# Two attention layers with adaptive norms on one core: the gates spread by high and low parts, a room check by lifetimes, and another order table

## The chip, the cores and the metric

The kernel runs on one core of one Trainium2 chip. The metric is the device time of one execution in microseconds (us), read as the median of several runs; lower is better. The engines are TensorE (PE; PEld are its weight loads), VectorE (DVE), ScalarE (ACT), GpSimd (POOL) and SyncE (SP), which issues most of the transfers (DMA).

## The reference, cut to what matters

Two layers over x of 256 tokens by 1024 channels, all in F32. Each layer takes a shift, a scale and a gate from one conditioning vector c, applies a mixer (first a sparse attention with three branches, NSA, then a block attention, MoBA), and adds the gated result:

```python
cond = jax.nn.silu(c)
for i in range(DEPTH):                       # 2
    shift, scale, gate = jnp.split(cond @ ada_w[i] + ada_b[i], 3, axis=-1)
    h = rms_norm(x, norm_g[i]) * (1 + scale[:, None, :]) + shift[:, None, :]
    ...                                      # y = nsa_mixer(h, ...) or moba_mixer(h, ...)
    x = x + gate[:, None, :] * y

# both mixers, cut: projections of h, 16 heads of 64 in 4 groups, softmax attention, a gated output
q, k, v, z = split_cols(h @ w_in, ...)
q = partial_rope(rms_norm(q, q_g), cos, sin)
p = masked_softmax(q @ k * scale, mask)
o = p @ v
return (o * jax.nn.silu(z)) @ w_out
```

`gate` is one row of 1024 numbers for each layer. The first mixer has compressed keys and gates of its three branches besides.

## The kernel before

**Numbers as two parts.** The large products (h with `w_in`, the gated attention output with `w_out`) run in F32R, a type of TensorE that keeps fewer bits of an F32 number. For exactness each operand is cut into `hi` (the F32R cast, on ACT) and `lo` (the rest, a subtraction on DVE), and three products hi·hi, hi·lo and lo·hi are added up in PSUM. `parts_of` makes the two parts of a piece of weights; the tags `hi` and `lo` have four buffers each. Transposes, the softmax's products with values and the products for shift, scale and gate run on F32 operands.

**How the work is staged.** First comes the start: c, x and the first columns of `ada_w` and `w_in` are loaded in small pieces into tiles named `early`. c is transposed into `RT` and turned into `condz` (silu of c, one column for each block of 128 channels); shift and scale of layer 0 are products of `condz` with columns of `ada_w`; they make `HT`, the transposed h in two parts. Products with `w_in` give k, v and q; then the NSA attention by pairs of heads (`pair_a`: scores, masked maxima on DVE, exponentials on ACT, scaling on DVE, transposes on PE, products with values); the products with `w_out`; then the same for the second layer (`pair_b`). Beside the main line run `side` steps: shift and scale of layer 1, and the two gates.

**The gate.** `ada_gate(l)` sums the gate over the partitions' 128 channels at a time: a tile `gate` of 128x1024 is cleared, its first partition gets the bias, and eight `scalar_tensor_tensor` on DVE add a block of `ada_w`, scaled by a column of `condz`. What then is missing is the sum over the 128 partitions, and that on all of them: a product with `ones`, a 128x128 tile of 1.0, in two halves of 512 columns. Both operands are F32. ACT copies the result from PSUM back to `gate`, where `x_update` reads it at the layer's end.

**The order.** Nothing runs in the order of the code. Every call is recorded by `Plan` with its dependencies; `Plan.issue` then writes out each engine's queue by simulating clocks: of the operations that are ready on an engine it takes the one that can start first, by level and then by its number (its place in the code). `LATER_BY` shifts numbers (first, last, shift), so it says what goes ahead of what; `HOLD` keeps single operations back until a planned time. Both are tables of plain numbers that belong to this code's numbering: an operation that is added moves all later numbers.

**Tiles.** A tag is a set of buffers of one size. `Plan.tile` gives names; `issue` hands out buffers as operations come. A tile may be given ahead of its turn only if `_safe` says that all tiles in between still find a buffer.

Of the kernel before, what the change touches and what calls it, by code (L numbers as in the profile page):

```python
# [10 lines left out]
F32R = mybir.dt.float32r  # L11
# [6 lines left out]
P = 128  # L18
# [21 lines left out]
ISSUE, FIRST_BYTE, RATE, LANDED = 450.0, 1500.0, 315.0, 700.0  # L40

LATER_BY = [
# [11 lines left out]
]  # L54
SHIFT = {i: d for a, b, d in LATER_BY for i in range(a, b + 1)}
HOLD = {
# [3 lines left out]
}  # L60


# [10 lines left out]
class Plan:  # L73
# [158 lines left out]
    @staticmethod  # L232
    def _safe(tag, k):

        if k not in tag.known:
            held = tag.early | {k}
            end = max(tag.last[h] for h in held)
            tag.known[k] = all(
                sum(a not in held and a not in tag.done for a in tag.alive[b]) + len(held) <= tag.bufs
                for b in range(tag.next, len(tag.tiles)) if b not in held and b not in tag.given and tag.first[b] <= end)  # L240
        return tag.known[k]

# [191 lines left out]
def kernel(  # L434
# [25 lines left out]
    const = ctx.enter_context(tc.tile_pool(name="const", bufs=1))  # L460
    work = ctx.enter_context(tc.tile_pool(name="work", bufs=1))
    psum = ctx.enter_context(tc.tile_pool(name="psum", bufs=1, space=bass.MemoryType.PSUM))
    plan = Plan(nc)
    T, A, V, G, Q = plan.T, plan.A, plan.V, plan.G, plan.S
# [97 lines left out]
        keep(maskC[:, m, :], [[-16, 16]], m * P - 31)  # L562
    ones = const.tile([P, P], F32, name="ones")
    nc.gpsimd.memset(ones, 1.0)
    identR = const.tile([P, P], F32R, name="identR")
    V.tensor_copy(identR, identF)
    emask = const.tile([P, 2], F32, name="emask")
# [186 lines left out]
    def ada_gate(l):  # L754
# [5 lines left out]
        for kk in range(8):  # L760
            w = ada_piece(l, kk, 2 * D, D)[:, 0, :]
            with plan.at(FILL):
                V.scalar_tensor_tensor(gate, w, condz[:, kk, 0:1], gate, op0=OP.mult, op1=OP.add)
            yield
        for s in range(2):
            t = tile_of("ps", 512)
            with plan.at(FILL):
                T.matmul(t, ones, gate[:, s * 512:(s + 1) * 512], start=True, stop=True)
                A.copy(gate[:, s * 512:(s + 1) * 512], t)

    side = []
# [792 lines left out]
```

## Time and profile before

| what | value |
|---|---|
| median of 3 runs | 308.93 us (308.55 to 309.64) |
| the profiled execution | 308.65 us |
| its span, first to last instruction | 306.9 us |
| busy: PE, PEld | 297.4 us (97%), 242.4 us (79%) |
| busy: DVE, ACT, POOL | 248.6 us (81%), 203.0 us (66%), 29.3 us (10%) |
| granted clock of TensorE | 1.000 over the span |
| DMA | 65.80 MB, mean 214 GB/s |

All instructions that the plan writes out stand under one line (L406 in this kernel), since a helper issues them; so rows are told apart by their tiles, `out<-in`, in which buffer numbers are left out. `acc` and `ps` are PSUM tiles, `p` and `pT` the probabilities and their transposes, `qg` holds q and later the gated outputs, `tiny` the maxima and sums of rows. A matmul's modelled end can lie behind the start of the next one, so lengths of neighbours overlap and starts tell the pace.

### The profile page before, as it was taken

To read this page: it belongs to the slowest core of one execution; us is meant where nothing else is said; L and a number is where in the kernel's file an instruction comes from. 1 tells how busy PE (TensorE), PEld (TensorE's weight loads), DVE (VectorE), ACT (ScalarE), POOL (GpSimd) and SP (SyncE) were. 2 spreads that over 40 slices of the span, in tenths; PEclk is the share of its full clock that TensorE was granted. 3 is DMA by queue.
4 is the path that set the end of the run, shared out by engine and by line. 5 is a ranking of instruction groups with operands and counts; after the bars stand their busy time and mean duration, and the time that the engine had idled before them with its cause. 6 is when DMAs were issued, how large, how long until landed. Compare 5 with 4: busy or idle time off the path is not lost.

```text
span 306.9 us, 6115 instructions
## 1 busy us (share of the span) xinstructions
PE 297.4 (97%) x2097; PEld 242.4 (79%) x2097; DVE 248.6 (81%) x737; ACT 203.0 (66%) x484; POOL 29.3 (10%) x100
## 2 busy tenths in 40 slices
PE   3999999999999999999999999999999999999995
PEld 3866767878878696878897788787788999878784
DVE  2773473678699989799999898796599999999664
ACT  4644254674946786689877975866466589999510
POOL 8028980000000000000000000000000000000000
PEclk9999999999999999999999999999999999999999
DMA  7999999699974294958568259126487780531002
GB/s 249 323 357 368 367 355 336 220 260 328 351 273 143 64 379 149 346 193 347 147 199 266 76 185 326 41 75 209 142 259 228 242 275 15 142 138 66 2 34 103
DMA packets 41099, 65.80 MB, mean 214 GB/s; under 512 B 4220, under 2 KB 20970, under 8 KB 41068
## 3 DMA queue, kind: packets, MB, share of 16 engines
q1 hardware_dynamic: 40708, 65.36, 65.0%
q8 instruction: 16, 0.26, 0.3%
q14 instruction: 15, 0.12, 0.1%
q10 hardware_dynamic: 168, 0.06, 0.1%
q0 software_dynamic: 192, 0.00, 0.0%
HBM read 64.36 MB, written 1.05 MB: 213 GB/s over the span
## 4 chain that ended last, share of the span: by engine, by line
PE 83%; DVE 5%; ACT 5%; DMA 3%; issue 2%; ACTq 1%; DVEq 0%
PE ps L406 48%; PE acc L406 36%; DVE p L406 3%; ACT p L406 2%; DMA rot<-in_c_dram 1%; DMA raw<-in_nsa_w_out_dram 1%; DVE lo L406 1%; ACT pT L406 1%; ACT hi L406 1%; ACTq L406 1%; ACT n_out L406 1%; DVE tiny L406 0%; ACT qg L406 0%; DVE n_out L406 0%; ACT y L406 0%
## 5 line engine op out<-in xcount | busy, mean ns | idle before, releaser
L406 ACT CAST hi<-raw 128x1024 fp32r<-128x1024 f32 (+1 forms) x48 | 49.2, 1027 | 17.4 <-PE acc L406 15.0
L406 DVE TENSOR_TENSOR lo<-raw,hi 128x1024 fp32r<-128x1024 f32 (+1 forms) x48 | 56.5, 1183 | 3.3 <-ACT hi L406 3.0
L406 ACT ACTIVATE p<-p,tiny 128x128 f32<-128x128 f32 (+1 forms) x96 | 43.2, 460 | 10.8 <-DVE tiny L406 10.6
L406 PE MATMUL acc<-hi,HT 128*128 128x512 f32 (+1 forms) x160 | 49.6, 383 | 0.1
L406 PE MATMUL acc<-HT,hi 128*128 128x256 f32 x192 | 39.0, 288 | 0.0
L406 PEld LDWEIGHTS acc<-hi,HT 128*128 128x128 f32 x160 | 28.8, 188 | 7.0 <-issue 1.2
L406 DVE CUSTOM_DVE_ANT_0 p<-ps,causal 128x128 f32<-128x128 f32 (+1 forms) x96 | 30.8, 346 | 1.6 <-PE ps L406 1.5
L406 PEld LDWEIGHTS acc<-HT,hi 128*128 128x128 f32 x192 | 30.4, 188 | 0.9 <-issue 0.7
L406 PE MATMUL acc<-lo,HT 128*128 128x512 f32 (+1 forms) x80 | 30.3, 382 | 0.2 <-DVE lo L406 0.2
L406 PE MATMUL ps<-hi,HT 128*128 128x512 f32 (+1 forms) x96 | 28.9, 367 | 0.0
L406 PE MATMUL ps<-KTA,qg 128*128 128x256 f32 (+2 forms) x192 | 27.3, 282 | 0.0
L406 PE MATMUL acc<-HT,lo 128*128 128x256 f32 x96 | 27.3, 286 | 0.0
L406 PEld LDWEIGHTS ps<-KTA,qg 128*128 128x128 f32 x192 | 24.1, 189 | 3.4 <-issue 1.2
L406 PE MATMUL ps<-hi,qg 128*128 128x256 f32 (+1 forms) x96 | 24.4, 324 | 0.0
L406 PE MATMUL acc<-hi,qg 128*128 128x512 f32 x64 | 23.3, 415 | 0.0
L406 ACT COPY pT<-ps 128x384 f32<-128x384 f32 x48 | 21.1, 493 | 2.3 <-PE ps L406 2.1
L406 DVE TENSOR_TENSOR lo<-early,hi 128x1024 fp32r<-128x1024 f32 (+2 forms) x17 | 17.3, 1038 | 5.1 <-ACT hi L406 4.7
L406 PE MATMUL ps<-identF,p 128*128 128x128 f32 x144 | 21.1, 275 | 0.2
L406 PEld LDWEIGHTS ps<-hi,HT 128*128 128x128 f32 x96 | 17.2, 188 | 4.6 <-issue 1.9
L406 DVE SCALAR_TENSOR_TENSOR gate<-raw,condz,gate 128x1024 f32<-128x1024 f32 x16 | 20.4, 1276 | 0.4 <-DMA raw<-in_ada_w_dram 0.4
L406 ACT CAST hi<-early 128x1024 fp32r<-128x1024 f32 (+2 forms) x17 | 14.6, 895 | 8.5 <-DMA early<-in_nsa_w_in_dram 6.7
L406 PEld LDWEIGHTS ps<-identF,p 128*128 128x128 f32 x144 | 16.2, 140 | 3.9 <-DVE p L406 1.0
(218 smaller groups left out, 617.7 us busy)
## 6 DMA issues: line engine op xcount, KB each, us to landing
raw<-in_ada_w_dram SPq DMA_DIRECT2D x32, 512.0 KB, 4.6
raw<-in_moba_w_in_dram SPq DMA_DIRECT2D x20, 512.0 KB, 4.4
early<-in_ada_w_dram SPq DMA_DIRECT2D x12, 512.0 KB, 10.1
raw<-in_nsa_w_in_dram SPq DMA_DIRECT2D x12, 512.0 KB, 6.1
early<-in_nsa_w_in_dram SPq DMA_DIRECT2D x9, 512.0 KB, 9.2
raw<-in_nsa_w_out_dram SPq DMA_DIRECT2D x8, 512.0 KB, 4.5
raw<-in_moba_w_out_dram SPq DMA_DIRECT2D x8, 512.0 KB, 4.2
early<-in_nsa_w_in_dram SPq DMA_DIRECT2D x9, 256.0 KB, 4.8
```

Source lines behind the costliest of these rows:

```text
L406: r = getattr(self.engines[e], method)(*[self._real(a) for a in args], **{k: self._real(a) for k, a in kw.items()})
```

## The change

1. `ada_gate` spreads the gate by parts: `parts_of` cuts `gate` (as two halves of 512) into `hi` and `lo` in F32R, and for each half two F32R products, of `hi` and of `lo` with `onesR`, add up in one PSUM tile, in place of one F32 product. `onesR` is a new F32R copy of `ones`, made once on DVE. So eight products stand for four; one cast on ACT and one subtraction on DVE are added for each layer, and one cast on DVE at the start.
2. `_safe` counts room by lifetimes: a tile that is held ahead of its turn counts at a place only if it comes behind that place or is alive there.
3. `LATER_BY` and `HOLD` are other tables.

```diff
 LATER_BY = [
-    (110, 111, -64), (256, 256, 155), (308, 311, -51), (317, 318, -56), (331, 331, 298), (351, 351, 26),
...
+    (162, 163, -25), (347, 347, 181), (443, 472, -10), (604, 604, 15), (634, 641, 236), (643, 645, 124),
...
 HOLD = {
-    0: 3500, 121: 16500, 168: 22100, 306: 52600, 313: 37600, 384: 32300, 386: 34800, 391: 48600, 396: 51100,
...
+    91: 18000, 95: 15300, 308: 19200, 310: 22300, 314: 36200, 389: 47600, 391: 50700, 605: 50800, 1251: 146800,
...
@@ _safe
-                sum(a not in held and a not in tag.done for a in tag.alive[b]) + len(held) <= tag.bufs
+                sum(a not in tag.done for a in tag.alive[b]) + sum(h > b for h in held) <= tag.bufs
@@
     ones = const.tile([P, P], F32, name="ones")
     nc.gpsimd.memset(ones, 1.0)
+    onesR = const.tile([P, P], F32R, name="onesR")
+    V.tensor_copy(onesR, ones)
@@ ada_gate
+        hi, lo = parts_of(gate.rearrange("p (s n) -> p s n", s=2))
         for s in range(2):
             t = tile_of("ps", 512)
             with plan.at(FILL):
-                T.matmul(t, ones, gate[:, s * 512:(s + 1) * 512], start=True, stop=True)
+                with plan.group():
+                    T.matmul(t, onesR, hi[:, s], start=True, stop=False)
+                    T.matmul(t, onesR, lo[:, s], start=False, stop=True)
                 A.copy(gate[:, s * 512:(s + 1) * 512], t)
```

The tables move instructions nearly everywhere. Three places follow, with the queue before and the queue now. A number behind a tile's name is its buffer.

ACT's queue at the start: `rot` is the tile into which c is loaded, `y` takes the rows of norms and biases, `sg` is the sigmoid of c, `n_in` and `ss` the squares of x and their sums. Before:

```order
L406 DMA y_135<-in_norm_g_dram 16x128
L406 DMA y_135<-in_ada_b_dram 48x128
L406 DMA y_135<-in_nsa_cmp_b_dram 4x128
L406 DMA y_135<-in_nsa_cmp_pe_dram 32x128
L406 DMA rot_151<-in_c_dram 8x128
L406 ACT_TABLE_LOAD
L406 ACTIVATE n_in_155,ss_156<-X 128x1024
L406 ACTIVATE n_in_166,ss_167<-X 128x1024
L406 ACTIVATE sg<-RT 128x8
```

Now:

```order
L403 DMA rot_136<-in_c_dram 8x128
L403 DMA y_140<-in_norm_g_dram 16x128
L403 DMA y_140<-in_ada_b_dram 48x128
L403 DMA y_140<-in_nsa_cmp_b_dram 4x128
L403 DMA y_140<-in_nsa_cmp_pe_dram 32x128
L403 ACT_TABLE_LOAD
L403 ACTIVATE sg<-RT 128x8
L403 ACTIVATE n_in_162,ss_163<-X 128x1024
L403 ACTIVATE n_in_174,ss_175<-X 128x1024
```

The transfer of c has gone from the fifth place to the first, and `sg` from behind both squares of x to ahead of them; on DVE `condz` goes ahead of the row norms in the same way, behind the new cast of `onesR`.

PE's queue at the second layer's gate, amid the products of z (`acc<-HT,hi`), of the output (`acc<-hi,qg`) and the attention's scores (`ps<-KTA,qg`) and transposes (`ps<-identF,p`). Before:

```order
L406 MATMUL acc_272<-HT,hi_331 128x256
L406 MATMUL ps_153<-gate_357,ones 128x512
L406 MATMUL ps_232<-identF,p_722 128x128
L406 MATMUL ps_232<-identF,p_734 128x128 x2
L406 MATMUL ps_198<-gate_357,ones 128x512
L406 MATMUL acc_299<-hi_297,qg_1306 128x512
```

Now:

```order
L403 MATMUL acc_281<-HT,hi_345 128x256 x2
L403 MATMUL acc_275<-hi_328,qg_1406 128x512
L403 MATMUL ps_154<-hi_248,onesR 128x512
L403 MATMUL ps_154<-lo_342,onesR 128x512
L403 MATMUL acc_281<-HT,lo_271 128x256
L403 MATMUL acc_281<-HT,hi_345 128x256
L403 MATMUL acc_275<-lo_369,qg_1406 128x512
L403 MATMUL acc_275<-hi_328,qg_1406 128x512 x2
L403 MATMUL ps_154<-KTA,qg_1571 128x128 x4
L403 MATMUL ps_243<-hi_248,onesR 128x512
L403 MATMUL ps_243<-lo_342,onesR 128x512
```

The two products of the gate have become two pairs, they stand behind the first output products, and no transpose of `p` stands between them any more.

DVE's queue ahead of that gate: the last sums of `gate`, between the scaling of `p`, the sums' reciprocals (`tiny`), and the gated outputs (`g`, `qg`). Before:

```order
L406 SCALAR_TENSOR_TENSOR gate_357<-raw_637,condz,gate_357 128x1024
L406 SCALAR_TENSOR_TENSOR g_1000<-zT_736,ps_207 128x256
L406 SCALAR_TENSOR_TENSOR g_1022<-zT_736,ps_173 128x256
L406 RECIPROCAL tiny_1202<-tiny_1202 128x4
L406 TENSOR_SCALAR tiny_926<-tiny_926 128x4
L406 SCALAR_TENSOR_TENSOR gate_357<-raw_616,condz,gate_357 128x1024
L406 TENSOR_TENSOR qg_1306<-g_1000,qg_1306 128x256
L406 TENSOR_TENSOR qg_1306<-g_1022,qg_1306 128x256
L406 TENSOR_SCALAR p_722<-p_722,tiny_1202 128x128 x2
L406 TENSOR_SCALAR p_734<-p_734,tiny_1202 128x256
L406 SCALAR_TENSOR_TENSOR zT_727<-y_202,acc_299 128x512
L406 SCALAR_TENSOR_TENSOR zT_741<-y_135,acc_272 128x512
```

Now, where `lo<-gate` follows five rows further on:

```order
L403 SCALAR_TENSOR_TENSOR gate_350<-raw_605,condz,gate_350 128x1024
L403 TENSOR_TENSOR qg_1406<-g_1002,qg_1406 128x256
L403 TENSOR_TENSOR qg_1406<-g_1023,qg_1406 128x256
L403 RECIPROCAL tiny_1148<-tiny_1148 128x4
L403 RECIPROCAL tiny_1155<-tiny_1155 128x4
L403 SCALAR_TENSOR_TENSOR gate_350<-raw_622,condz,gate_350 128x1024
L403 TENSOR_SCALAR p_720<-p_720,tiny_1148 128x128 x2
L403 TENSOR_SCALAR p_734<-p_734,tiny_1148 128x256 x2
L403 TENSOR_SCALAR p_727<-p_727,tiny_1155 128x128 x2
L403 TENSOR_SCALAR p_722<-p_722,tiny_1155 128x256 x2
L403 SCALAR_TENSOR_TENSOR gate_350<-raw_656,condz,gate_350 128x1024
L403 TENSOR_TENSOR lo_369<-raw_650,hi_328 128x1024
```

Three sums of the gate stand here now, where two stood; the products with z (`zT`) have moved behind them.

More of the change, by code (lines that the diff above doesn't have):

```diff
@@ L56 @@
 HOLD = {
[3 rows of a table removed]
+    91: 18000, 95: 15300, 308: 19200, 310: 22300, 314: 36200, 389: 47600, 391: 50700, 605: 50800, 1251: 146800,
+    1389: 167700, 1528: 190600, 1546: 192800, 1570: 198600, 1578: 202000, 1649: 209300, 2314: 282300,
 }
```

20 rows, old and new, of tables (HOLD, LATER_BY) are left out of this document.

## The prediction

> **What bounds the kernel now.** I read the page first, for the shares of the engines, then the chain that ended last, then the busy time by stretches, and last the timeline at the two gates, at the start and at the end. Ahead of all: the profiled execution took 308.65 us, its span is 306.9 us, so 1.75 us lie around the span; the median of the three runs is 308.93 us, 0.28 us above the profiled one. I make the sum against 308.65 and add the 0.28 at the end. About 0.3% of the median, 0.93 us, is what a measurement of this kernel can tell from no change.
>
> From the page, its first line, three engines, and the shares of the chain:
>
> ```profile
> span 306.9 us, 6115 instructions
> PE 297.4 (97%) x2097; PEld 242.4 (79%) x2097; DVE 248.6 (81%) x737; ACT 203.0 (66%) x484; POOL 29.3 (10%) x100
> PEclk9999999999999999999999999999999999999999
> PE 83%; DVE 5%; ACT 5%; DMA 3%; issue 2%; ACTq 1%; DVEq 0%
> ```
>
> TensorE (PE) is busy in 297.4 of 306.9 us, at the full granted clock in every slice, and 83% of the last chain is its own work. Where it is idle, the waits and the chain in order of time say:
>
> ```profile
> PE ps L406 <- DMA X<-in_x_dram: 4.3, 1, 4.3
> PE ps L406 <- DMA rot<-in_c_dram: 0.8, 1, 0.8
> 300.46 2.86 PE ps L406 x24
> 303.34 0.44 DVE y L406
> ```
>
> 4.3 and 0.8 us at the start and 3.6 us behind its last matmul (303.3 to 306.9) are 8.7 of the 9.5 idle us. So between 7.1 and 303.3 us PE has hardly a hole, and time goes down by what is taken off PE, as long as the other engines keep it fed. "Busy" hides short stalls, though: a matmul's modelled end stretches over them. The weight loads (PEld) show them:
>
> ```profile
> PEld ps L406 <- issue: 10.4, 32, 0.8
> PEld acc L406 <- issue: 3.1, 11, 0.8
> PEld ps L406 <- DVE tiny L406: 2.3, 6, 0.8
> PEld ps L406 <- ACT p L406: 1.2, 2, 0.8
> PEld ps L406 <- DVE gate L406: 0.8, 1, 0.8
> ```
>
> No single one is over 0.8 us. The other rival for the bound is VectorE (DVE), in two stretches:
>
> ```profile
> 150.00:160.00 10.00, 10.00 (x87) 9.00 (x86) 10.00 (x35) 7.38 (x24) 0.00 (x0) 1.00 0.60 185
> 160.00:170.00 10.00, 10.00 (x72) 7.93 (x71) 10.00 (x32) 8.35 (x29) 0.00 (x0) 1.00 0.77 245
> 250.00:260.00 10.00, 10.00 (x93) 9.95 (x92) 10.00 (x46) 9.64 (x29) 0.00 (x0) 1.00 0.29 104
> 260.00:270.00 10.00, 10.00 (x78) 8.04 (x76) 10.00 (x35) 10.00 (x35) 0.00 (x0) 1.00 0.53 153
> 280.00:290.00 10.00, 10.00 (x74) 7.99 (x75) 8.37 (x31) 7.07 (x20) 0.00 (x0) 1.00 0.01 2
> ```
>
> Columns are length, then busy us of PE, PEld, DVE, ACT and POOL. DVE is full (10.00 of 10) there and PE is too: both feed each other, with no slack on either. The next rows show that the gates are spread in just these stretches.
>
> **The gate products.** Four of them, two for each layer: the instructions that read `gate` (first and last start at 167.1 and 268.6 us), the timeline at the second gate, and rows of full-width products of the F32R kind near the end:
>
> ```profile
> L406 PE MATMUL ps<-gate,ones x8: 592/592/697, 167.1 to 268.6; 128*128 128x512 f32 x8
> 266.94 1.02 PE L406 MATMUL ps<-gate,ones 128*128 128x512 f32 x2
> 267.80 0.58 PE L406 MATMUL ps<-identF,p 128*128 128x128 f32 x3
> 292.06 2.80 PE acc L406 x12
> 297.66 2.80 PE acc L406 x12
> ```
>
> Eight records for four products: a product of F32 operands takes two passes. From the start of the pair to the start of what follows, 267.80 - 266.94 = 0.86 us a product. Twelve F32R products of the same width (`acc<-hi,qg` and `acc<-lo,qg`, 128x512) take 2.80 us, 0.233 each. The change puts two of these, high and low, for one of the old: 0.467 for 0.86, 0.39 saved, four times: 1.57 us less work on PE. Since PE has no holes there, I count all of it: -1.6 us. Its ends: nothing, if PE waits at the spot anyway, and -1.6.
>
> The Trainium skill, page "TensorE: Matmul & The Clock Gate", section "Back-to-back issue gap", states about 131 ns a matmul for N=512 as the sustained rate in a stream of loads and matmuls, and about 216 ns for an isolated gap. By 131 ns the eight new products would cost 1.05 us in place of 3.44, and the term would be -2.4 us, the time 306.3 us. The trace's 233 ns stand near the second figure and not the first, so the row decides and the sum stays with it.
>
> **The new casts and differences.** `parts_of` on a gate is one cast on ScalarE (ACT) and one subtraction on DVE over 128x1024, and at the start `onesR` is cast once:
>
> ```profile
> L406 ACT CAST hi<-raw 128x1024 fp32r<-128x1024 f32 (+1 forms) x48 | 49.2, 1027 | 17.4 <-PE acc L406 15.0
> L406 DVE TENSOR_TENSOR lo<-raw,hi 128x1024 fp32r<-128x1024 f32 (+1 forms) x48 | 56.5, 1183 | 3.3 <-ACT hi L406 3.0
> L406 DVE SCALAR_TENSOR_TENSOR gate<-raw,condz,gate 128x1024 f32<-128x1024 f32 x16 | 20.4, 1276 | 0.4 <-DMA raw<-in_ada_w_dram 0.4
> ```
>
> Two casts of 1.03 us on ACT and two differences of 1.18 us on DVE: +2.1 and +2.4 us. They lie beside PE, which has products of z and of the output to run; but DVE is full in both stretches, and in the second one the new order has three gate sums of 1.28 us in the last stretch where two stood, so DVE gets 1.18 + 1.28 = 2.5 us more ahead of the last heads. If the cover held fully this costs nothing; with no cover 2.5 us here and 1.2 at the first gate, 3.7 in all. It holds nearly: at 280 to 290 DVE has room again (8.37), and PE still has output products then. I take +0.2, near the lower end, because the row of waits ending with DVE's gate is 0.8 us in one place today. What else queues: behind the difference on DVE stand the scaling of the probabilities and the masked maxima of the next pair; PE's transposes wait for those. One buffer each of `hi` and `lo` (four of each) is held for the gate, for its cast, difference and products (some 3 us); weights then have three for that time. That is in the same +0.2. `onesR` is one 128x128 cast at the head of DVE's queue, priced with the start.
>
> **The start.** The order now issues c first on ACT's queue, where it stood fifth, and forms `sg` and `condz` ahead of the row norms. Rows of the start, and the landing of the DMA that is first now:
>
> ```profile
> 0.81 0.41 ACTq L406 DMA_DIRECT2D y<-in_norm_g_dram  x1
> 2.68 0.34 ACTq L406 DMA_DIRECT2D rot<-in_c_dram  x1
> 4.18 0.20 POOL L564 MEMSET ones<- 128x128 f32 x1
> 4.35 1.06 ACT L406 ACTIVATE n_in<-X 128x1024 f32<-128x1024 f32 x1
> 7.12 0.27 PE L406 MATMUL ps<-identF,rot 8*128 8x8 f32 x1 [0.80 <-DMA rot<-in_c_dram]
> 8.28 0.47 DVE L406 TENSOR_SCALAR n_in<-X,rs 128x512 f32<-128x512 f32 x1
> 8.74 0.17 DVE L406 TENSOR_TENSOR condz<-sg,RT 128x8 f32<-128x8 f32 x1
> 9.49 1.50 PE L406 MATMUL ps<-early,condz 128*32 128x128 f32 x32
> 13.30 0.49 PE L406 MATMUL acc<-hi,HT 128*128 128x512 f32 x1
> GB/s 249 323 357 368 367 355 336 220 260 328 351 273 143 64 379 149 346 193 347 147 199 266 76 185 326 41 75 209 142 259 228 242 275 15 142 138 66 2 34 103
> ```
>
> c's issue moves from 2.68 to about 0.81, 1.87 us earlier, so it lands at about 7.1 - 1.9 = 5.2 us. `onesR` waits for the memset that ends at 4.4 and holds the queue's head, `identR` and the reduction behind it, but not beyond that. So `condz` can stand at about 6.5 us, not 8.9. It is of use only when the first columns of `ada_w` are there: x (1.05 MB), the rows (0.05) and those columns (1.05) are 2.15 MB; at 249 GB/s for the first 7.7 us (1.92 MB) and 323 then, 8.4 us. The first products on `condz` could start some 0.5 to 1.0 us before 9.49. Against it: ACT now does `sg` ahead of both squares of x, which move from 4.35 to about 5.8, 1.4 us; the row norms (`n_in` at 8.28) keep perhaps half of that, since they lose a wait for c in their middle. The first product at 13.30 needs both sides. Ends: 1.0 earlier, 0.7 later; I take -0.3. The weights come at 357 to 368 GB/s from then to 38 us, so a part of what is won here is waited for at the next landing.
>
> **The other order and the room check.** Every queue's order changes beyond these places. No new instruction comes from it. What it could take away is bounded by the stalls that the loads show, 17.8 us in the five rows, of which most are short steps that any order has (43 at 13.5 us, 0.31 each); the rows that end with DVE or ACT, 4.3 us, are what an order moves. It can as well add as much. I take 0 and keep -2 and +2, half of 4.3, for the range. The check that lets a tile be given ahead of its turn counts differently, so it may start transfers earlier or later; its price is in the same term. The end has a price of its own. Behind the last values of attention PE ran 19 rows of other output products before it came to those of the last pair; now 4 rows stand there (five products, 5 x 0.233 = 1.2 us). What the last pair needs in that time, from before:
>
> ```profile
> 289.21 0.50 PE L406 MATMUL acc<-lo,qg 128*128 128x512 f32 x1
> 289.74 0.98 DVE L406 TENSOR_TENSOR qg<-g,qg 128x256 fp32r<-128x256 f32 x2
> 289.85 0.41 ACT L406 CAST qg<-g 128x256 fp32r<-128x256 f32 x1 [0.31 <-DVE g L406]
> ```
>
> The values end as the first of these rows starts, at 289.2; the last difference is there at 290.7, 1.5 us later. Five products and the first two of the last pair, which read only the cast, cover 1.6 us. So the wait is 0 to 0.2 us, and I put it at nothing.
>
> **Sum.** -1.6 (gates) + 0.2 (their parts) - 0.3 (start) + 0 (order) = -1.7: 308.65 - 1.7 = 306.95 in the profiled execution's terms, 307.2 beside the median.
>
> **Rivals.**
>
> A: DVE decides the second attention (slower). At 250 to 270 us it is full, and 2.5 us are added ahead of the last heads. If PE runs out of products there, the end moves by 2.5 less the 1.6 and 0.3 won, +0.6, and with 1.2 at the first gate +1.8: 309.5 to 310.7, middle 310.1. It decides as soon as more than 1.9 us of the 3.7 show as waits of PE. For it: DVE 10.00 in four rows above. Against: PE has the output products to run, and DVE is down to 8.37 at 280.
>
> B: the saved passes turn into waits at the gate (no change). PE's gate product must now wait for sum, cast, difference, 1.28 + 1.03 + 1.18 in a chain, where it waited for the sum alone; if the order puts it too early, the queue behind it stands. PE stands in order, so a wait of 1.6 us in all eats the gain, with the other two terms at -0.1: 308.8 us. For it: the 0.8 us wait on DVE's gate today. Against: a transposition or a product can stand ahead, as the second gate's rows show.
>
> C: the order takes out waits too, -2 of the 4.3 us: 305.2 us. For it: gates of both sides no longer run at F32's slow pace inside a full stretch, and the start's 1.0. Against: nothing in the trace says that such an order exists.
>
> D: the change doesn't do what it says: that the pair costs as much as the two old passes. Each row of F32R products here, 2.80 us for twelve, speaks against it; 308.8 us too.
>
> **Chances.** My forecast (306.2 to 308.0): 0.50; A 0.13; B 0.15; C 0.19; D 0.03. Faster by over 0.3% (below 308.0): the forecast and C, 0.69, less the forecast's upper edge, 0.67. Within 0.3% (308.0 to 309.9): B, D and that edge, 0.20, and the lower end of A less what the order's +2 could add to B: 0.21. Slower: 0.12, the rest of A and that tail. The range leaves out half of C's lower side and most of A: 305.0 to 309.3. The likeliest case has a range of 306.2 to 308.0 of its own.
>
> **What would show it.** Right: eight records of `ps<-hi,onesR` and `ps<-lo,onesR` with 0.23 us from start to start; PE's busy time down by 1.5 to 2 us and its idle still some 9; the `identF,rot` product at 5.3 us and not 7.1, and the first `acc<-hi,HT` at 12.3 to 13.3; DVE's busy time up by 2 to 3 us. Wrong: a row among PEld's waits on DVE `lo` or ACT `hi` of over 1 us near the gates; a hole in PE behind 270 us; a first product later than 13.5; or the stalls by "issue" up by more than 2 us, which would be the order's doing.

## The result, and the profile after

| kernel | median of 6 runs | ratio to before, 95% interval | profiled execution | its span |
|---|---|---|---|---|
| before | 309.55 us (308.55 to 309.64) | 1 | 308.65 us | 306.9 us |
| after | 311.22 us (309.48 to 312.51) | 1.0062 [1.0035, 1.0088] | 309.80 us | 308.1 us |

The change made the kernel slower by 0.6%, where 307.2 us had been forecast. Three more executions moved before's median from 308.93 to 309.55 us, so its profiled execution lies 0.9 us under the median. Three of the six runs of after had a granted clock of 0.994 to 0.995 (311.8 to 312.5 us) and the other three, the profiled one among them, 0.998 to 1.000 (309.5 to 310.7 us), so the traces explain a loss of 1.15 us (309.80 against 308.65) and not the whole of the median's 1.7.

The page of after: its first line, the engines, the rate of the transfers in 40 slices of 7.7 us, and the chain's shares.

```profile
span 308.1 us, 6115 instructions
PE 298.2 (97%) x2097; PEld 242.5 (79%) x2097; DVE 252.0 (82%) x740; ACT 205.9 (67%) x486; POOL 31.2 (10%) x100
GB/s 250 322 356 368 366 355 332 218 160 346 263 399 87 126 174 297 223 329 293 124 176 237 150 203 340 127 68 202 86 276 261 274 205 0 200 211 1 3 20 116
PE 78%; DVE 12%; DMA 5%; issue 2%; ACT 1%; SPq 1%; ACTq 0%; DVEq 0%
```

DVE is busy 3.4 us longer than before, ACT 2.9. PE's busy time went up by 0.8 us and not down by 1.5 to 2: a matmul's modelled end stretches over short stalls, so the sum hides what the gates saved. In the chain PE has lost 5 points and DVE has won 7. The ninth slice of the transfers (61.6 to 69.3 us) fell from 260 to 160 GB/s. PE's waits, and three of its weight loads':

```profile
PE ps L403 <- DMA rot<-in_c_dram: 2.9, 1, 2.9
PE ps L403 <- DMA X<-in_x_dram: 1.2, 1, 1.2
PE ps L403 <- DVE rs L403: 0.9, 1, 0.9
PE ps L403 <- DMA p<-in_nsa_cmp_w_dram: 0.8, 1, 0.8
PEld ps L403 <- issue: 13.5, 39, 1.3
PEld acc L403 <- issue: 2.1, 6, 0.8
PEld ps L403 <- DMA p<-in_nsa_cmp_w_dram: 1.6, 2, 1.1
```

The row on `cmp_w`, the compression's weights, is new; "issue" has grown by 2.1 us (10.4 and 3.1 before). The start, in order of time:

```profile
0.81 0.58 ACTq L403 DMA_DIRECT2D rot<-in_c_dram  x1
2.86 0.24 PE L403 MATMUL ps<-identF,rot 8*128 8x8 f32 x1 [2.86 <-DMA rot<-in_c_dram]
4.27 3.36 PE L403 MATMUL ps<-X,identF 128*128 128x128 f32 x14 [1.17 <-DMA X<-in_x_dram]
4.42 0.93 DVE L403 CAST onesR<-ones 128x128 fp32r<-128x128 f32 x1 [4.42 <-POOL ones L561]
6.16 0.17 DVE L403 TENSOR_TENSOR condz<-sg,RT 128x8 f32<-128x8 f32 x1
7.56 1.09 PE L403 MATMUL ps<-early,condz 128*32 128x128 f32 x16
14.43 0.48 PE L403 MATMUL acc<-hi,HT 128*128 128x512 f32 x1
```

c is there at 2.9 us, `condz` at 6.2 and its first products at 7.56, all earlier than forecast; yet the first product with weights starts at 14.43, 1.1 us later than before's 13.30. The second place is at 74 us:

```profile
73.97 0.44 PE L403 MATMUL acc<-hi,HT 128*128 128x304 f32 x2
75.25 1.59 PE L403 MATMUL ps<-p,p 128*64 128x256 f32 x7 [0.84 <-DMA p<-in_nsa_cmp_w_dram]
```

PE stands for a piece of the compression's weights that is still on the wire. At the second gate, at 278 us, and in the stretch behind it there is no such hole:

```profile
L403 PE MATMUL ps<-hi,onesR x4: 392/394/451, 174.2 to 278.2; 128*128 128x512 f32 x4
278.25 0.45 PE L403 MATMUL ps<-hi,onesR 128*128 128x512 f32 x1
278.54 0.39 PE L403 MATMUL ps<-lo,onesR 128*128 128x512 f32 x1
278.77 0.40 PE L403 MATMUL acc<-lo,qg 128*128 128x512 f32 x1
280.00:290.00 10.00, 10.00 (x70) 8.42 (x69) 9.24 (x34) 9.36 (x25) 0.00 (x0) 1.00 0.01 2
```

**Three marks on PE** tell where the time went: the first product `acc<-hi,HT`, the last `ps<-zT,p` (end of the compression), and the last matmul. The second mark is the end of the span in these rows, of before and then of after:

```profile
L406 PE MATMUL ps<-zT,p x32: 379/379/379, 67.3 to 85.2; 128*64 128x256 f32 x32
```
```profile
L403 PE MATMUL ps<-zT,p x32: 379/379/379, 68.4 to 87.7; 128*64 128x256 f32 x32
```

For every kernel of this study (us; the starts of these three matmuls in its trace, and the differences):

| kernel | first `acc<-hi,HT` | to last `zT,p` | last `zT,p` | to last matmul | last matmul |
|---|---|---|---|---|---|
| before | 13.30 | 71.85 | 85.15 | 217.87 | 303.02 |
| after | 14.43 | 73.30 | 87.73 | 216.43 | 304.16 |
| after_again | 12.89 | 75.15 | 88.04 | 216.28 | 304.32 |
| after_f32gate | 12.88 | 74.44 | 87.32 | 218.01 | 305.33 |
| after_605late | 14.44 | 73.45 | 87.89 | 216.44 | 304.33 |
| after_unblocked | 12.88 | 75.73 | 88.61 | 216.58 | 305.19 |
| after_spare | 12.90 | 73.65 | 86.55 | 216.35 | 302.90 |
| before_newstart | 12.84 | 71.97 | 84.81 | 218.21 | 303.02 |
| first75_from_before | 14.11 | 72.64 | 86.75 | 216.57 | 303.32 |
| first160_from_before | 14.53 | 71.26 | 85.79 | 216.16 | 301.95 |
| first160_f32gate | 14.08 | 70.99 | 85.07 | 217.41 | 302.48 |
| both | 12.75 | 71.38 | 84.13 | 216.04 | 300.17 |
| gate_only | 14.33 | 71.05 | 85.38 | 223.02 | 308.40 |
| gate_late | 14.41 | 71.29 | 85.70 | 219.72 | 305.42 |
| gate_left_out | 14.02 | 71.89 | 85.91 | 217.76 | 303.67 |

Behind 88 us after is 1.44 us quicker than before, about what was forecast for the gates. Ahead of it after loses 2.58 us, 1.13 up to the first product and 1.45 between that and the compression's end. The 1.13 us belong to these two traces and not to the change: before's 13.30 is the earliest of the seven kernels with the old start (the others have 14.02 to 14.53), and after_again, the same kernel as after, has 12.89. The experiments ask for the rest.

### The profile page after: what moved, and what is told of

Same layout as the page of the kernel before. It is cut to its first block, busy times and chain, and to the rows that moved or that the text cites. A ratio compares the mean times of both kernels' runs of the same rounds, so it can differ in the third digit from the quotient of the medians.

```text
span 308.1 us, 6115 instructions
## 1 busy us (share of the span) xinstructions
PE 298.2 (97%) x2097; PEld 242.5 (79%) x2097; DVE 252.0 (82%) x740; ACT 205.9 (67%) x486; POOL 31.2 (10%) x100
## 4 chain that ended last, share of the span: by engine, by line
PE 78%; DVE 12%; DMA 5%; issue 2%; ACT 1%; SPq 1%; ACTq 0%; DVEq 0%
PE ps L403 46%; PE acc L403 32%; DVE p L403 3%; DVE lo L403 3%; DVE gate L403 2%; DMA p<-in_nsa_cmp_w_dram 2%; DMA y<-in_ada_b_dram 2%; DMA early<-in_ada_w_dram 1%; SPq L403 1%; DVE tiny L403 1%; ACT hi L403 1%; DVE n_out L403 1%; DVE pc L403 0%; DVE zT L403 0%; DVE rot L403 0%
## 5 line engine op out<-in xcount | busy, mean ns | idle before, releaser
L403 DVE CUSTOM_DVE_ANT_0 p<-ps,causal 128x128 f32<-128x128 f32 (+1 forms) x96 | 29.9, 347 | 2.5 <-PE ps L403 2.3
L403 PE MATMUL ps<-hi,HT 128*128 128x512 f32 (+1 forms) x96 | 27.9, 367 | 0.2 <-ACT hi L403 0.2
L403 PE MATMUL ps<-KTA,qg 128*128 128x256 f32 (+2 forms) x192 | 28.0, 282 | 0.1
L403 PE MATMUL ps<-identF,p 128*128 128x128 f32 x144 | 22.1, 277 | 0.0
L403 PE MATMUL acc<-hi,qg 128*128 128x512 f32 x64 | 22.1, 398 | 0.0
```

The source lines that it names most:

```text
L403: r = getattr(self.engines[e], method)(*[self._real(a) for a in args], **{k: self._real(a) for k, a in kw.items()})
```

## The experiments

Most of these kernels keep a given order on every queue: a list of operation numbers, one for each pick, stands in place of the planner's choice, so that single rows can be moved and all others stay.

```diff
-            start, _, _, op, e = best
+            op = ops[ORDER[done]]
+            e = op["engine"]
```

The expectations stand as they were written, with the theories then held. On the gates: the pairs save what they take off PE, or the saving turns into waits. On the order: theory W says that the order holds SP's queue at 64 us behind a piece that has no free buffer, so that the wire stands and the compression's weights come late; the rival is that something else in the tables costs the time.

### The gates by themselves

**gate_only**: before's order on every queue, with pairs in the places of the F32 products; the cast and the difference stand right behind the last sum of each gate and write into two spare tiles.

```diff
+        hi, lo = parts_of(gate.rearrange("p (s n) -> p s n", s=2),
+                          (tile_of("n_parts", KP, 512), tile_of("n_parts", KP, 512)))
-                T.matmul(t, ones, gate[:, s * 512:(s + 1) * 512], start=True, stop=True)
+                with plan.group():
+                    T.matmul(t, onesR, hi[:, s], start=True, stop=False)
+                    T.matmul(t, onesR, lo[:, s], start=False, stop=True)
```

> The order of before, row for row, with the gate's parts set in: one cast on ACT and one difference on DVE right behind each layer's last gate sum, two F32R products at each place of an F32 product, and onesR cast on DVE at 22 us. The parts lie in tiles that are free there (n_parts), not in the weights' hi and lo. Theory O (the gates' saving was right, the new order lost more than it): 1.5 to 1.7 us faster than before, ratio 0.9945 to 0.995, since eight products of 0.233 us replace eight passes of 0.43. Rival G (the gate's chain of sum, cast and difference eats the saving as waits): within 0.5 us of before or slower.

Measured: 314.59 us, 1.0159 [1.0137, 1.0181]. Its timeline at the first gate, PE, ACT and DVE:

```profile
163.21 1.04 ACT L503 CAST n_parts<-gate 128x1024 fp32r<-128x1024 f32 x1 [0.81 <-DVE gate L503]
164.16 0.47 ACT L503 COPY pT<-ps 128x384 f32<-128x384 f32 x1
164.68 0.74 PE L503 MATMUL ps<-KTA,qg 128*128 128x256 f32 x4 [1.40 <-ACT pT L503]
```

ACT stands 0.81 us for the last sum, the copy of transposes waits behind the cast, and PE waits 1.40 us for that copy: the cast delays PE through a neighbour in ACT's queue. The part behind the compression takes 223.02 us against 217.87.

**gate_late**: as gate_only, but the casts, differences and pairs of both gates stand further back, where DVE has room (in the trace gate 1's pairs start at 176 and 181 us, gate 2's at 292 and 293).

> The order of before again with the gate's parts set in, now where the engines have room: the first layer's cast on ACT in the place of the old copy, its difference in DVE's idle stretch at 173 us, its products at 175 and 179 us; the second layer's cast and difference behind the last weight parts at 287 and 288 us, its products at 291 us. Nothing else moves. Theory O: the eight passes of 0.43 us go and eight products of 0.233 come, 1.6 to 1.8 us faster than before, ratio 0.994 to 0.995; the 5 us that the parts cost right behind the sums were their place alone. Rival G (the parts cost DVE and ACT time that PE waits for in any place): ratio 0.999 or more.

Measured: 310.93 us, 1.0043 [1.0031, 1.0055]. Where the first gate's products had stood, PE waits for the scaled probabilities:

```profile
168.57 0.40 PE L503 MATMUL acc<-lo,qg 128*128 128x512 f32 x1
170.25 0.70 PE L503 MATMUL ps<-identF,p 128*128 128x128 f32 x3 [1.28 <-DVE p L503]
```

So at the first gate the slow F32 products had stood in time that PE would have waited for DVE. The part behind the compression is 1.85 us longer than before's (219.72 against 217.87); that is about what eight products of 0.233 us add in new places, if nothing is won in the old ones, an estimate that no run tests.

**gate_left_out**: before's order and operations, but the four products have 2 columns, so the sum over the partitions is left out.

```diff
-                T.matmul(t, ones, gate[:, s * 512:(s + 1) * 512], start=True, stop=True)
-                A.copy(gate[:, s * 512:(s + 1) * 512], t)
+                T.matmul(t[:, 0:2], ones, gate[:, s * 512:s * 512 + 2], start=True, stop=True)
+                half = gate[:, s * 512:(s + 1) * 512]
+                A.copy(half, half)
```

> The order of before with the spreading of the gates left out: each F32 product is cut from 512 to 2 columns and ACT copies the gate onto itself instead of the product, so the gate is not summed over the partitions. PE has 3.0 us less to do in four places (4 x 0.86 less some 0.1), nothing else changes. The step of the prediction that counted all work taken off PE at those places: 3.0 us faster, ratio 0.990. Theory D, from the waits of 1.44 us at 168 us and 1.4 us at 268 us that stand on PE when the products are moved away (DVE and ACT work up to there sets the pace, PE's F32 products fill the time): at most 1 us faster, ratio 0.997 or more.

Measured: 309.16 us, 0.9986 [0.9975, 0.9997]. Some 3 us of PE's work are gone, and 0.4 us of time. At the second gate:

```profile
260.00:270.00 10.00, 9.33 (x79) 8.04 (x77) 10.00 (x38) 10.00 (x35) 0.00 (x0) 1.00 0.44 139
```

PE has 0.67 us of open holes now in a stretch where DVE and ACT are full (10.00 each). In before's order these two set the pace there, and PE's gate products were filling.

**after_f32gate**: after's order on every queue, casts and differences too, but F32 products of `gate` and `ones` in the pairs' places.

```diff
-                with plan.group():
-                    T.matmul(t, onesR, hi[:, s], start=True, stop=False)
-                    T.matmul(t, onesR, lo[:, s], start=False, stop=True)
+                with plan.group(hi, lo, after=(n, n + 1)) as op:
+                    T.matmul(t, ones, gate[:, s * 512:(s + 1) * 512], start=True, stop=True)
+                    op["cost"] = 2 * 512 * 1.07
```

> The changed kernel with its order kept on every engine, its casts and differences of the gate too, but the four gate products again on F32 operands (gate and ones). Theory O: 1.6 us slower than the changed kernel, ratio to before about 1.011 where the changed kernel had 1.006. Rival G: as the changed kernel, 1.006, since PE waited at the gate anyway. Rival C (the changed kernel's runs are longer because TensorE's granted clock is lower in them, 0.994 to 0.998 in four of six, and not because of its order): the longer F32 products make no difference that can be told from the clock's, and the granted clock is under 0.998 here as well.

Measured: 310.97 us, 1.0054 [1.0031, 1.0077]. The ratio of 1.011 that was expected is missed, and beside after's first median (311.22) the pairs are worth nothing. Against after_again below (310.00) they are worth 1.0 us, with intervals that overlap; by the marks it is 218.01 - 216.28 = 1.7 us behind the compression, and the gain in after's places rests on these marks. Without the pairs, after's order behind 88 us takes what before's takes (218.01 and 217.87).

### The order

**after_again**: after once more, without an edit, with 12 runs.

> The changed kernel once more, beside the others on the same chip, because three of its first six runs stood at a granted clock of 0.994 to 0.995. Theory O (its order costs): the ratio to before stays at 1.004 to 1.008 whatever the clock shows. Rival C (the clock): at a clock of 0.998 or more the ratio falls to 1.001 to 1.003.

Measured: 310.00 us, 1.0021 [1.0002, 1.0041]: the loss is smaller than at first, and still there. The two traces of this one kernel differ at the start. First of after, then of after_again:

```profile
9.57 1.09 PE L403 MATMUL ps<-identF,n_in 128*128 128x128 f32 x4 [0.93 <-DVE rs L403]
10.76 1.08 PE L403 MATMUL ps<-early,condz 128*32 128x128 f32 x16
```
```profile
9.55 0.63 PE L403 MATMUL ps<-identF,n_in 128*128 128x128 f32 x4 [0.96 <-DVE rs L403]
10.20 0.64 PE L403 MATMUL ps<-early,condz 128*32 128x128 f32 x16
```

The same four transposes at the same time take 1.09 us or 0.63: PE is still at half pace in the first trace. That is the 1.5 us by which the first product differs (14.43, 12.89). But the compression ends at 87.73 and 88.04: the early start is lost again on the way, so PE's work does not set that end in after's order.

**before_newstart**: before without the entry that held c's transfer back, which gives after's start: c first, `condz` ahead of the row norms.

```diff
-    0: 3500, 121: 16500, 168: 22100, 306: 52600, 313: 37600, 384: 32300, 386: 34800, 391: 48600, 396: 51100,
+    121: 16500, 168: 22100, 306: 52600, 313: 37600, 384: 32300, 386: 34800, 391: 48600, 396: 51100, 500: 79600,
```

> Before with one entry of HOLD taken out (0: 3500), so that c's transfer goes first on ACT's queue, and the sigmoid and condz ahead of the row norms; every queue is as before from 16 us on. The prediction put such a start at 0.3 us faster. Theory O, from the trace of the changed kernel, where the first product of the weights started at 14.43 and not 13.30 us: the first product about 1 us later, most of it taken back before 50 us, since the weights' transfers set the pace there; 0 to 0.6 us slower, ratio 1.000 to 1.002. If the whole start counts: 1.1 us slower, ratio 1.0036.

Measured: 309.00 us, 0.9991 [0.9972, 1.001]. The first product stands at 12.84 and not 13.30, and the whole does not change measurably; the interval leaves room for up to 0.9 us.

**first75_from_before**: before's order for what starts ahead of 75 us, after's behind it.

> The changed kernel with the order of before up to 75 us (all that before issues up to there, the first four blocks of the compression's products among it), and the changed kernel's order for the rest. Theory O with its place: the wait of PE for the compression's weights at 74 us (1.0 and 0.4 us, and what follows) came from the order ahead of it, where the casts of four weight pieces start 4.9 us later on ACT and so hold SP's queue; without it the time falls by 2.0 to 2.9 us to a ratio of 0.997 to 0.9995. Rival L (the loss is spread over the later order): ratio 1.004 or more. Rival C (granted clock): 1.004 or more, with a clock of 0.994 to 0.998.

Measured: 309.12 us, 0.9985 [0.9973, 0.9997]. PE stands 1.28 us at 80 us for ACT's copy `n_in` out of PSUM, at the end of a chain in which ACT had stood 2.06 us for a piece of `w_in`. Neither before nor after has a hole there, so it is put down to the joint. With it the kernel is 0.9 us quicker than after_again; without it that would be 2.2, an estimate, and then most of what after's order costs lies ahead of 75 us.

**first160_from_before**: the same with the joint at 160 us, so that only the two gates' part and all behind it is after's.

> The order of before up to 160 us (all that before issues up to the first gate's products), and the changed kernel's order for the rest, gates by parts included. Theory O (what is lost lies ahead of 160 us, and the gates' saving holds): 1.3 to 1.8 us faster than before, ratio 0.994 to 0.996. Rival L (the later order loses as well, the late first gate or the denser end): ratio 0.999 or more.

Measured: 307.40 us, 0.9926 [0.9914, 0.9938]. No stall at the joint, a compression stretch of 71.26 us like before's, and 216.16 us behind it like after's.

**first160_f32gate**: that kernel with F32 products, as in after_f32gate.

> The kernel with the order of before up to 160 us and the changed order behind it, its order kept on every engine, casts and differences too, but the four gate products on F32 operands (gate and ones). Theory O (where the new order puts the gates, PE's work sets the pace): 1.3 to 1.7 us slower than with F32R pairs, ratio 0.997 to 0.9985 where the pairs had 0.9926. Rival W (PE waits there anyway, and the later order alone is what gains): ratio 0.993 to 0.994.

Measured: 308.11 us, 0.9951 [0.9938, 0.9964]. The pairs are worth 0.7 us here by the medians and 217.41 - 216.16 = 1.25 by the marks; the rest of the gain over before's median, 1.5 us, belongs to the order behind 160 us, of which the marks show 0.5 behind the compression, against a trace of before that is itself 0.9 us under its median.

**after_605late**: one row of after moved on SP's queue: the piece of `ada_w` goes behind the four pieces of `cmp_w` that follow it.

> The changed kernel with one row of SP's queue moved: the piece of ada_w that waits for a raw buffer at 66 us (issued at 67.67) goes behind the four pieces of the compression's weights; every other row and every other queue stays. Theory O with its place: those pieces are issued and land up to 1.5 us earlier, the waits of 1.0 and 0.4 us at 74 us go, and the kernel is 1.0 to 1.4 us faster than the changed one, ratio to before 1.001 to 1.003. Rival L: the end does not move, since a later landing is waited for instead; ratio 1.005 to 1.007.

Measured: 308.62 us, 0.9972 [0.9958, 0.9985], 1.4 us quicker than after_again. The profiled run was its slowest, at 309.96 us, and there the wait has only moved on, to that very piece:

```profile
75.25 1.03 PE L503 MATMUL ps<-zT,p 128*64 128x256 f32 x8
78.02 1.06 PE L503 MATMUL ps<-raw,condz 128*32 128x512 f32 x8 [1.75 <-DMA raw<-in_ada_w_dram]
```

Its first product is one of the late ones too (14.44). What made the other runs quicker that trace can't tell.

**after_unblocked**: the SP row and PE's products on it (`ps<-raw,condz`) moved some 5 us back, so that nobody should wait for that piece.

> The changed kernel with two rows moved: on SP's queue the piece of ada_w behind the four pieces of the compression's weights, as before, and on PE the group of products that reads this piece (ps from raw and condz at 77.5 us) behind the next compression group, some 5 us later, because the profile with the first move alone showed a wait of 1.94 us there. Theory O with its place (the late transfers at 66 to 78 us are the loss): neither wait shows, and the time falls by 1.5 to 2.5 us against the changed kernel, ratio 0.994 to 0.997. Rival L (further losses lie between 80 and 160 us): ratio 0.998 or more.

Measured: 310.58 us, 1.0029 [1.0014, 1.0045]. No gain. The wire stands as before, and another wait comes up at the next place, 1.84 us at 79.3. It ends with ACT's copy `n_in` out of PSUM, which starts at 78.86, when DVE's row `tiny` ahead of it is done:

```profile
64.00:68.00 4.00, 4.00 (x27) 2.88 (x27) 2.66 (x6) 3.61 (x10) 0.00 (x0) 1.00 0.44 130
79.29 0.50 PE L503 MATMUL acc<-hi,HT 128*128 128x512 f32 x1 [1.84 <-ACT n_in L503]
80.00:84.00 4.00, 4.00 (x22) 2.82 (x22) 1.99 (x7) 3.52 (x9) 0.00 (x0) 0.58 1.04 363
```

The last number of a window's row is the rate, the third from the end the granted clock. 64 to 68 us has 130 GB/s, so the wire was still half idle: moving the wait's place did not help. And behind the new wait TensorE's clock falls: 0.58 over these 4 us means some 3.4 us at half clock, in which PE was busy all the time, so up to 1.7 us of this trace (an estimate) were lost to the clock and not to the order.

**after_spare**: after's order row for row, but the piece of `ada_w` goes into a buffer of another tag (`n_out`) that is free at that time, so SP need not hold it back.

```diff
+        own = self.tiles["raw.181"]
+        own["tag"].tiles.remove("raw.181")
+        own["tag"] = self.tags["n_out"]
+        own["tag"].tiles.append("raw.181")
```

> The changed kernel, order kept row for row on every engine, with one buffer more for one load: the piece of ada_w that is issued at 67.67 us, when a raw buffer comes free, goes into an n_out tile that is free there, so SP's queue has nothing to wait for at 64 us. Theory W (the wire stands half idle from 64 to 68 us, 134 to 167 GB/s where before has 284, because SP's queue is held by a raw buffer; half a megabyte is late from then on, and whichever piece goes last is waited for): 64 to 68 us carries 250 GB/s or more, the waits at 74 us go without another in their place, and the kernel is 1.2 to 2.0 us faster than the changed one, ratio 0.996 to 0.998 (the changed one was at 1.0021 and 1.0062). Rival L (the waits are not from that gap): they move on as in the two runs with rows moved, ratio 1.001 or more.

Measured: 308.88 us, 0.9982 [0.997, 0.9994], 1.1 us quicker than after_again. SP's queue in before, in after and here (start, length, transfer):

```profile
64.01 2.40 SPq L406 DMA_DIRECT2D raw<-in_nsa_w_in_dram  x2
67.48 0.88 SPq L406 DMA_DIRECT2D p<-in_nsa_cmp_w_dram  x2
```
```profile
63.52 0.88 SPq L403 DMA_DIRECT2D zT<-in_nsa_cmp_w_dram  x2
67.67 0.35 SPq L403 DMA_DIRECT2D raw<-in_ada_w_dram  x1
69.21 0.93 SPq L403 DMA_DIRECT2D p<-in_nsa_cmp_w_dram  x2
```
```profile
63.65 0.46 SPq L507 DMA_DIRECT2D n_out<-in_ada_w_dram  x1
66.88 0.37 SPq L507 DMA_DIRECT2D raw<-in_nsa_w_in_dram  x1
67.83 0.88 SPq L507 DMA_DIRECT2D p<-in_nsa_cmp_w_dram  x2
```

In after SP issues nothing from 64.4 to 67.67 us. What it waits for are the parts of the pieces that fill `raw`: a cast on ACT, and behind it a difference on DVE, whose end frees the buffer. The first of them in before and in after:

```profile
61.25 0.72 ACT L406 CAST hi<-raw 128x608 fp32r<-128x608 f32 x1
63.19 0.79 DVE L406 TENSOR_TENSOR lo<-raw,hi 128x608 fp32r<-128x608 f32 x1
```
```profile
66.13 0.69 ACT L403 CAST hi<-raw 128x608 fp32r<-128x608 f32 x1
66.85 0.79 DVE L403 TENSOR_TENSOR lo<-raw,hi 128x608 fp32r<-128x608 f32 x1 [1.05 <-ACT hi L403]
```

The differences end at 63.98 and 67.64 us, and SP's next transfers into `raw` start at 64.01 and 67.67.

The rates from 64 to 68 us, of before, after and after_spare:

```profile
64.00:68.00 4.00, 4.00 (x32) 3.09 (x30) 2.49 (x4) 3.59 (x9) 0.00 (x0) 1.00 0.96 284
```
```profile
64.00:68.00 4.00, 4.00 (x25) 3.17 (x25) 2.18 (x6) 3.33 (x9) 0.00 (x0) 1.00 0.55 167
```
```profile
64.00:68.00 4.00, 4.00 (x27) 2.94 (x27) 2.66 (x6) 3.61 (x10) 0.00 (x0) 1.00 0.87 255
```

284, 167 and 255 GB/s: between before and after 117 GB/s x 4 us = 0.47 MB are missing, 1.4 us at the 332 GB/s at which after moves them from 72 to 76 us. With one buffer more the wire is busy, the compression ends at 86.55 us where it was 87.73 and 88.04, and 1.1 us come back, a little less than W's 1.2 to 2.0. W holds for that part. It is not all: SP now stands at its next piece of `raw` till 66.88, PE still waits 0.62 us for `cmp_w`, and 86.55 is 1.4 us behind before's 85.15, from an earlier first product.

### Both good parts together

**both**: first160_from_before with after's start, c first.

> The best version so far, the order of before up to 160 us and the changed order behind it, with the start of the changed kernel (c's transfer first, condz ahead of the row norms) set in. The start alone gave a ratio of 0.9991 with an interval of 0.9972 to 1.001, so this is expected within 0.5 us of the version without it: ratio 0.991 to 0.994. If the later first product counts: 0.995 or more.

Measured: 305.96 us, 0.9879 [0.9866, 0.9891]: 3.7 us quicker than before and 4.0 than after_again, the best of all. The start is worth 1.45 us on top of first160_from_before, more than the 0.5 us that the expectation allowed; the compression's stretch (71.38 us) is before's and the part behind (216.04) is after's. From after_again this kernel differs only in the order ahead of 160 us, with c first in both kernels, and 3.9 of the 4.0 us lie ahead of the compression's end (84.13 against 88.04).

## Why the prediction was wrong, by its own steps

- **The gates, -1.6: right in size, and right where the change puts them.** The slowest pair takes 278.77 - 278.25 = 0.52 us from start to start, 0.47 was forecast. After and after_f32gate differ by 1.6 us behind the compression (216.43, 218.01), which is the term. But the reason given, "Since PE has no holes there, I count all of it", failed: in before's order gate_left_out took away nearly twice as much and gained 0.4 us. A full PE beside a full DVE meant that short stalls were hidden in "busy". It was after's order that let the gain through, with the gate's products at 174 and 276 to 278 us and not at 167 and 268.
- **Their parts, +0.2: within the order of after, about right.** No wait of PE on the gates' `hi` or `lo` reaches 1 us, and there is no hole behind 270 us. The price is the place's, though: 5 us in gate_only, where the forecast's bound was 3.7.
- **The start, -0.3: mis-sized.** c's transfer was issued 1.87 us earlier as reckoned, but landed at 2.9 us, not 5.2; that it no longer shares the wire with what stood ahead of it is the likely reason, not tried. The first product was put at 12.3 to 13.3: of the traces of after's order four have 12.9, and two, after's own and after_605late's, 14.4, where PE was at half pace for longer. What the start is worth by itself was 1.45 us in one pair of kernels and nothing measurable in another (before_newstart). In after's order it was worth nothing: the end of the compression did not follow it. Six of the eight traces with the new start have their first product at 12.75 to 12.90 us, six of the seven with the old one at 14.02 to 14.53, so in most traces the gain at that mark was 1.1 us or more and not 0.3.
- **The other order, 0 and at most +2: the step that failed.** It took from the waits that end with DVE or ACT (4.3 us) what an order can move, and put that at 0. The order ahead of 160 us alone, with c first in both kernels, cost 4.0 us (after_again against both). What after's order moved was a wait on neither of them: casts of `raw` 5 us later, a transfer without a buffer at the head of SP's queue, a wire at 167 GB/s, and PE waiting for weights at 74 us. One spare buffer brought 1.1 of the 4.0 us back. From the first product to the compression's end after's order takes 73.3 to 75.2 us (four traces; after_spare's 73.65 and after_unblocked's, with its half clock, aside), before's order there 71.0 to 72.0. That is 1.3 to 4.2 us, and "issue" was up by 2.1 us, which the prediction had named as the sign of it.
- **The end, 0 to 0.2: right.** Nothing waits there.
- **Rivals.** A (DVE decides the second attention) is not seen in after. B (saved passes become waits) is what gate_late and gate_left_out show in before's order, and not what made after slow. C (the order takes out waits) came true in part for the order behind 160 us: 0.5 us by the marks, 1.5 by the medians. D is refuted by 0.52 us a pair. The true case, an order that starves the wire ahead of the first attention, was in no rival; the sentence that the room check "may start transfers earlier or later" came near it, without a price of its own.
- **A slip in a sum.** With the 131 ns a product that the prediction tries out, its own numbers give 306.4 us (307.2 less 0.8) and not 306.3; the forecast does not use it.

**What stays open**: the other 1.4 us or more between after_spare and before's order in the same stretch, where, the 0.62 us for `cmp_w` aside, no hole of PE is longer than 0.26 us; whether the tables or the room check put SP's queue in that order, which no run separates; why after_605late gained 1.4 us; and why the early start paid 1.45 us in both and at most 0.9 in before_newstart.

## What to carry to other kernels

Cut the span at two or three marks on the bound engine and compare the pieces: here a gain of 1.4 us and a loss of 2.6 showed side by side, where the total told only their difference. Take several traces of a kernel for it: the first mark alone moved by 1.5 us between two traces of after. A rewritten order must be read on the transfer queue as well: look for a transfer at its head whose buffer is freed late, and for a slice in which the rate drops. And before work taken off a full engine is counted, look which other engine is full in the same stretch; there the saving is worth little until the order is changed as well.

## What the runs showed of the hardware that was not expected

PE runs at half pace at the start, for a time that differs from run to run, and the clock in the rows of windows does not show it (1.00 in those stretches). Neighbouring 128x128 F32 transposes start 213 ns apart at first and 109 ns later. In seven traces with the old start full pace comes at 10.5 to 13.5 us, in six of eight with the new one at 7.6 to 9.7; in after only at 13.9, and in after_605late it comes at 7.7 and is gone again at 9.6. With the new start PE has 30 matmuls without a hole from 4.27 to 8.65 us, while in before it stood for c at 7 us. But these figures are from after's trace, where full pace came last of all, so the missing hole alone does not decide it. The Trainium skill, page "TensorE: Matmul & The Clock Gate", section "Part 1: The HAM clock gate (the "warmup" mystery)", says that TensorE starts at half its clock and is let up after a window of about 3.4 us in which it was busy, that this window runs freely, and that the moment therefore differs between runs; the traces agree on the half pace and on a moment that differs between runs, and they give the price: 1.5 us at the first product of one and the same kernel.

Half clock can come back in the middle of a kernel. In after_unblocked a hole of 1.84 us at PE was followed by some 3.4 us at half clock (0.58 granted over 80 to 84 us), which brought the mean clock of that run to 0.994, close to that of three of after's first runs, whose traces were not kept. A hole alone does not do it: after_605late's 1.75 us at 78 us and after_again's 1.71 at 75.5 were not followed by such a stretch (1.00 from 76 to 84 us).
